# A hybrid decoder block on one core: the value products dealt out in three steps, and the state space kernels on four column tiles

## The chip, the cores and the metric

The program runs on one core of one Trainium2 chip. Its engines are TensorE (PE, with its weight load PEld), VectorE (DVE), ScalarE (ACT), GpSimd (POOL) and SyncE (SP, which starts most of the loads). The metric is the device time of one execution in microseconds. The kernel before takes 1155.02 us, the median of three runs (1151.35 to 1155.62).

## What is computed

The block takes 512 positions of width 1024, with 16 learned meta positions put in front (528 in all). Cut to what matters here:

```
h = concat(meta_tokens, x)
h = h + 0.5 * swiglu(rmsnorm(h), w1, w3, w2)              # first feed-forward
q, k, v, u, g_attn, g_ssm = split(rmsnorm(h) @ w_in)
attn = sliding_window_attention(q, k, v, sinks)           # 4 key groups x 4 query heads,
                                                          # blocks of 128, window 128, 16 meta keys
y    = s5_ssm(u, ...)                                     # 32 groups of 16 channels, 64 complex states
ssm  = (gelu(y) @ glu_a) * sigmoid(gelu(y) @ glu_b)
h = h + (sigmoid(g_attn) * attn + sigmoid(g_ssm) * ssm) @ w_out
h = h + 0.5 * swiglu(rmsnorm(h), ...)                     # second feed-forward
out = rmsnorm(h)[:, 16:]
```

In a query block of the attention, softmax runs over the 16 meta keys, up to 256 keys of the band and a sink; the value product is `p @ v` over those keys. The state space layer is computed in chunks of 8 steps; within a chunk its outputs come from a kernel of eight taps for each group, 16 by 16 channels each, which depends on the parameters alone.

## The kernel before

**Precision.** Weights and activations are split into a high and a low part (`whi`, `wlo`; `hgh`, `hgl`), and each large product is three matmuls for each 128 rows of the inner dimension (L238, L412, L414). ACT makes `whi` (L173) and DVE `wlo` (L174) from the weights as loaded (`raw`), in pieces of 128 output columns, by `prep_piece`. One piece feeds one *unit*: the 24 matmuls of 8 inner blocks. A unit's result (`p`) is taken out of PSUM by its evacuation, which is recorded in the next unit.

**Order.** Every engine runs its instructions in the order in which the program records them; nothing is scheduled behind it. Other work is put between a unit's matmuls by hand: `accumulate` takes a list of callbacks and runs them at equal distances in the unit. In the attention there are `NCUT = 11` such places in a unit, called cuts here and numbered 0 to 10; cut c stands behind matmul 2(c+1) of 24 (in a `glu` unit, which has two sums of 12, at about the same places).

**The state space kernels.** `ssm_params` is a generator whose steps run one in each unit of the first feed-forward. For each of four batches b of eight groups (`GB = 8`), it makes the kernel taps `Kt` (L651 to L658): for each group one matmul with the 128 x 16 stationary operand `BB` and the 128 x 128 moving operand `Qt` (L656), four of them into the rows 0 to 15 of one PSUM tile `psK`, side by side; one ACT copy of 16 x 512 (L658); then the same for the other four groups in the next step. Behind that POOL adds the diagonal (L663), and eight DMAs lay `Kt` out (L666).

**The attention.** Between projections, gates and glu units (30 units, table `MIX`) run 16 attention blocks n, key group k = n // 4 and query block b = n % 4. Block n begins in unit `BEGIN[n]`, and its parts stand in three units, at cuts given in the table `CUT`:
- In the first, `s1` for the four heads h at the cuts 2, 4, 7 and 7: two score matmuls `ps_s` (L1165, L1166), on DVE the mask and row minimum `mn` (L1168), on ACT the exponential `E` (L1170); behind head 3 the sum `den` and its reciprocal (DVE), and the scaling of `E` on POOL (L1181).
- In the second, at cut 7, `s2` turns the probabilities (`ps_t`, L1189; one or two sets of four) and splits them into `ph` (ACT, L1192) and `pl` (DVE, L1193). At cut 8, `s2m` turns the meta part (`ps_tm`, L1208), splits it (`ms`), and POOL spreads it into `m` (L1213). `prep_piece` is at cut 8 too, behind it.
- In the third, at cut 5, `s3` (L1217): the products of the band with `ph` and `pl` (L1224, two or four matmuls), the product of the meta part with `VM` (L1226), all into the PSUM tile `pv`; then ACT copies the lower half to `tb` (L1228), and DVE adds the halves into `AT` (L1230, two instructions).

The three parts of different blocks meet in one unit, in the order s3, s1, s2 where they share a cut. `ps_s` and `ps_tm` share two PSUM tiles, and `pv` has one:

```
1075    pt_ps = pool("ps_pt", 2, space=PSUM, c=ps3)
1076    pv_ps = pool("ps_pv", 1, space=PSUM, c=ps3)
```

Of the kernel before, what the change touches and what calls it, by code (L numbers as in the profile page):

```python
# [8 lines left out]
F32 = mybir.dt.float32  # L9
F32R = mybir.dt.float32r  # L10
AF = mybir.ActivationFunctionType
# [26 lines left out]
PREPS = (6, 34)  # L38
KS1 = 8
VS = (1, 0, 2, 10, 13, 13)  # L40
CUT = {"s3": 5, "s1": (2, 4, 7, 7), "s2o": 7, "s2p": 7, "s2m": 8, "prep": 8, "ev": 0, "ks": 10, "vs": 7}
BEGIN = (1, 2, 3, 4, 6, 7, 10, 11, 13, 14, 15, 18, 19, 20, 21, 24)

NG = 32
# [1 line left out]
GB = 8  # L46
NB = NG // GB
T = 8
# [17 lines left out]
def hybrid_block_kernel(  # L66
# [30 lines left out]
    V, S, G, PE, SY = nc.vector, nc.scalar, nc.gpsimd, nc.tensor, nc.sync  # L97
# [361 lines left out]
    Qt = pers.tile([128, NG, T + 1, 16], F32, name="Qt")  # L459
# [12 lines left out]
    def ssm_params(ps_p):  # L472
# [107 lines left out]
        ps = ps_p.tile([128, 512], F32, tag="ax", name="ps7")  # L580
# [13 lines left out]
        for i in range(2):  # L594
            ps = ps_p.tile([128, 512], F32, tag="ax", name="psA")
# [7 lines left out]
        BB = pp.tile([128, 2, NG, 16], F32, name="BB")  # L603
# [32 lines left out]
        for b in range(NB):  # L636
            gsl = slice(GB * b, GB * b + GB)
            tq = pp.tile([128, GB, T + 1, 16], F32, tag="s4", name="tq", bufs=2)
            G.tensor_tensor(out=Qt[:, gsl], in0=lam(LR, b, T + 1), in1=vec(A, 0, b, T + 1), op=ALU.mult)
            G.tensor_tensor(out=tq, in0=lam(LI, b, T + 1), in1=vec(A, 1, b, T + 1), op=ALU.mult)  # L640
            yield
            G.tensor_tensor(out=Qt[:, gsl], in0=Qt[:, gsl], in1=tq, op=ALU.add)
            Pb = pp.tile([128, GB, T, 16], F32, tag="s4", name="Pb", bufs=2)
            G.tensor_tensor(out=Pb, in0=lam(LR, b, T), in1=vec(BB, 0, b, T), op=ALU.mult)
            yield
            tq = pp.tile([128, GB, T, 16], F32, tag="s4", name="tq", bufs=2)
            G.tensor_tensor(out=tq, in0=lam(LI, b, T), in1=vec(BB, 1, b, T), op=ALU.mult)
            G.tensor_tensor(out=Pb, in0=Pb, in1=tq, op=ALU.add)
            yield
            yield  # L650
            Kt = pp.tile([16, GB, T, 16], F32, tag="s4", name="Kt", bufs=2)  # L651
            for h in range(2):
                ps = ps_p.tile([128, 512], F32, tag="ax", name="psK")
                for i in range(4):
                    g = GB * b + 4 * h + i
                    PE.matmul(out=ps[:16, 128 * i:128 * i + 128], lhsT=BB[:, 0, g, :],  # L656
                              rhs=Qt[:, g, 0:T, :].rearrange("p t c -> p (t c)"), start=True, stop=True)
                S.activation(out=Kt[:, 4 * h:4 * h + 4].rearrange("p g t c -> p (g t c)"), in_=ps[:16, :], func=AF.Copy)  # L658
                yield
            dg = pp.tile([16, GB, 16], F32, tag="dg", name="dg")  # L660
            G.tensor_tensor(out=dg, in0=ident[:16, 0:16].unsqueeze(1).to_broadcast([16, GB, 16]),
                            in1=dT[:, gsl].unsqueeze(2).to_broadcast([16, GB, 16]), op=ALU.mult)
            G.tensor_tensor(out=Kt[:, :, 0, :], in0=Kt[:, :, 0, :], in1=dg, op=ALU.add)  # L663
            for s in range(T):
                r0 = 16 * (T - 1 - s)
                G.dma_start(out=Mt[r0:r0 + 16, gsl, 16 * s:128],  # L666
                            in_=Kt[:, :, 0:T - s, :].rearrange("p g t c -> p g (t c)"))
            for h in range(2):
                ps = ps_p.tile([128, 512], F32, tag="ax", name="psW")
                for i in range(4):  # L670
                    PE.transpose(ps[:, 128 * i:128 * i + 128], Pb[:, 4 * h + i].rearrange("p t c -> p (t c)"), ident)
                S.activation(out=Wt[:, GB * b + 4 * h:GB * b + 4 * h + 4, :].rearrange("p g c -> p (g c)"), in_=ps, func=AF.Copy)
                yield
# [7 lines left out]
        for b in range(NB):  # L681
# [5 lines left out]
            n = 1  # L687
# [46 lines left out]
    ps = ax_ps.tile([128, 512], F32, tag="ax", name="ps_w")  # L734
    for _ in range(WARM):
        PE.matmul(out=ps[:, 0:128], lhsT=ones, rhs=ones, start=True, stop=True)
    ps = ax_ps.tile([128, 512], F32, tag="ax", name="ps_g")
# [106 lines left out]
    units, _ = ffn_units(hg, hT, True, mm_ps, g_p, t_p, CHUNKS1, norm_hook(t_p, hT, hg2, 1), first_mm)  # L844
# [237 lines left out]
    VM = a_p.tile([128, 4, 128], F32R, name="VM")  # L1082
# [5 lines left out]
    def tmp(name):  # L1088
        return a_p.tile([128, 512], F32, tag="t", name=name, bufs=4)
# [127 lines left out]
    def s3(n):  # L1217
        k, b = divmod(n, 4)
        _, _, tiles, ms = att.pop(n)
        pv = pv_ps.tile([128, 512], F32, tag="pv", name="pv")  # L1220
        first = True
        for ph, pl, kb in tiles:
            for p in (ph, pl):
                PE.matmul(out=pv, lhsT=VB[:, kb, k, :], rhs=p, start=first, stop=False)  # L1224
                first = False
        PE.matmul(out=pv, lhsT=VM[:, k, :], rhs=ms.rearrange("p h c -> p (h c)"), start=False, stop=True)  # L1226
        tb = tmp("tb")
        S.activation(out=tb[0:64], in_=pv[64:128, :], func=AF.Copy)  # L1228
        for e in range(2):
            V.tensor_tensor(  # L1230
                out=AT[64 * e:64 * e + 64, 2 * k:2 * k + 2, 128 * b:128 * b + 128],
                in0=pv[0:64].rearrange("p (i e c) -> p e i c", e=2, c=128)[:, e],
                in1=tb[0:64].rearrange("p (i e c) -> p e i c", e=2, c=128)[:, e], op=ALU.add)
# [57 lines left out]
    begin = dict(zip(BEGIN, range(16)))  # L1291
    for i, u in enumerate(units):
        cuts = [[] for _ in range(NCUT)]

        def at_cut(c, f, *a):
            cuts[c].append(lambda: f(*a))

        if i - 2 in begin:
            at_cut(CUT["s3"], s3, begin[i - 2])
        if i in begin:  # L1300
            for h in range(4):
                at_cut(CUT["s1"][h], s1, begin[i], h)
        if i - 1 in begin:
            for f, c in ((s2o, "s2o"), (s2p, "s2p"), (s2m, "s2m")):
                at_cut(CUT[c], f, begin[i - 1])
        at_cut(CUT["ev"], flush)
        if i == KS1:
            at_cut(CUT["ks"], ksplit, 1)
            at_cut(CUT["ks"], vmeta, 1)
        for v, iv in enumerate(VS):  # L1310
            if i == iv:
                at_cut(CUT["vs"], vsplit, *divmod(v, 3))
        at_cut(CUT["prep"], prep_piece)
        if i == len(units) - 2:
            mg += new_hg(SEQ)
            for m in range(6):
                at_cut(m, msplit, m)

        step(*u, mids=[lambda fs=fs: [f() for f in fs] for fs in cuts], prep=False, hold=i < len(units) - 1)
# [59 lines left out]
    n = CHUNKS2[-1]  # L1379
# [55 lines left out]
    ps = [new_p() for _ in range(2)]  # L1435
# [4 lines left out]
    for j in range(2 * ND):  # L1440
        h, d = divmod(j, ND)
        prep_piece()
        if j < 2:
            p = ps[j]
        else:
            p = new_p()
# [43 lines left out]
```

## Time and profile before

| what | value |
|---|---|
| three runs | 1151.35, 1155.02, 1155.62 us |
| the profiled execution's own time | 1151.97 us |
| its span, first to last instruction | 1150.2 us |
| granted TensorE clock, mean | 0.998 |
| busy: PE, PEld, DVE, ACT, POOL | 1130.5, 1006.9, 632.7, 408.8, 360.5 us |
| first feed-forward (span 0 to about 431 us) with the state space kernels | `psK` matmuls from 137.6 to 292.8 us |
| attention stage | about 510 to 716 us |

The profile is of one execution. Times are microseconds from the start of the span unless marked ns. "Busy" of PE is modelled at the matmul's end, since matmuls overlap, so starts are the safer reading: the pace of a stream is the distance from start to start. A plain float32 matmul shows as two records with a weight load each, a split (float32r) one as one. The waits view names the instruction that waited, the one that let it go, the total, the count and the longest.

### The profile page before, as it was taken

Reading aid. Unit: us, or ns where it says so; the run is one execution under the profiler, and the core shown is the slowest. Engines: PE = TensorE matmul, PEld = TensorE weight load, DVE = VectorE, ACT = ScalarE, POOL = GpSimd, SP = SyncE. Lnnn points to the kernel's source line nnn. Section 1 sums busy time; section 2 is a strip of 40 time slices with the busy share of each in tenths; the row PEclk is TensorE's granted clock in tenths of the full one; section 3 lists DMA queues with packets and bytes.
Section 4 is the critical chain, followed back from the end, with each engine's and each line's share of the span. In section 5 each row is a group of like instructions: output and inputs, shape, how many; then the busy total and the mean of one; then the engine's idle time right before and its main releaser. Section 6 shows DMA issues by size and latency. Waiting matters only on the chain.

```text
span 1150.2 us, 17220 instructions
## 1 busy us (share of the span) xinstructions
PE 1130.5 (98%) x7006; PEld 1006.9 (88%) x7006; DVE 632.7 (55%) x960; ACT 408.8 (36%) x719; POOL 360.5 (31%) x488
## 2 busy tenths in 40 slices
PE   9999999999999999999999999999999999999997
PEld 7999999999999999977777778888888888888887
DVE  5446653645444463877777776564544444444454
ACT  5322222232222242456555554343322321322234
POOL 2957672543685031444453331021000000000003
PEclk9999999999999999999999999999999999999999
DMA  6423233232423146122212222432323223323222
GB/s 186 99 90 107 74 93 109 77 85 83 111 74 102 62 141 204 49 74 74 72 45 69 74 74 74 147 110 74 128 92 110 74 83 120 112 70 126 76 74 74
DMA packets 105583, 108.43 MB, mean 94 GB/s; under 512 B 7504, under 2 KB 101968, under 8 KB 105376
## 3 DMA queue, kind: packets, MB, share of 16 engines
q1 hardware_dynamic: 103104, 100.74, 27.9%
q0 software_dynamic: 2352, 6.52, 2.2%
q8 instruction: 55, 0.90, 0.3%
q14 instruction: 24, 0.20, 0.1%
q10 hardware_dynamic: 48, 0.07, 0.0%
HBM read 100.80 MB, written 5.34 MB: 92 GB/s over the span
## 4 chain that ended last, share of the span: by engine, by line
PE 86%; DVE 5%; ACT 4%; issue 2%; POOL 2%; DMA 0%; POOLq 0%; DVEq 0%; SPq 0%; ACTq 0%
PE p L238 58%; PE p L412 11%; PE p L414 9%; PE p L798 1%; ACT E L1170 1%; PE p L1385 1%; POOL m L1213 1%; POOL E L1181 1%; DVE wlo L174 1%; PE psK L656 1%; ACT whi L173 1%; PE ps_x L744 1%; PE ps_t L1189 1%; ACT qs L1142 0%; PE pv L1224 0%
## 5 line engine op out<-in xcount | busy, mean ns | idle before, releaser
L238 PE MATMUL p<-hgh,whi 128*128 128x264 f32 (+1 forms) x1408 | 403.3, 333 | 0.1
L238 PE MATMUL p<-hgl,whi 128*128 128x264 f32 (+1 forms) x1408 | 402.3, 332 | 0.0
L238 PE MATMUL p<-hgh,wlo 128*128 128x264 f32 (+1 forms) x1408 | 400.6, 331 | 0.0
L174 DVE TENSOR_TENSOR wlo<-raw,whi 128x1024 fp32r<-128x1024 f32 (+2 forms) x192 | 256.4, 1336 | 105.0 <-ACT whi L173 102.7
L238 PEld LDWEIGHTS p<-hgh,whi 128*128 128x128 f32 x1408 | 238.6, 188 | 25.8 <-issue 1.5
L238 PEld LDWEIGHTS p<-hgh,wlo 128*128 128x128 f32 x1408 | 238.2, 188 | 23.4
L238 PEld LDWEIGHTS p<-hgl,whi 128*128 128x128 f32 x1408 | 238.4, 188 | 22.3
L173 ACT ACTIVATE whi<-raw 128x1024 fp32r<-128x1024 f32 (+2 forms) x192 | 187.5, 979 | 132.5 <-PE p L414 72.2
L1401 POOL TENSOR_TENSOR acc<-acc,zq 128x256 f32<-128x256 f32 x12 | 8.8, 735 | 349.9 <-ACT zq L1394 349.7
L384 ACT ACTIVATE t<-t 128x528 f32<-128x528 f32 (+1 forms) x44 | 28.1, 639 | 164.2 <-DVE t L383 164.2
L394 ACT ACTIVATE gh<-t 128x528 fp32r<-128x528 f32 (+1 forms) x44 | 28.1, 639 | 159.5 <-DVE t L393 159.5
L432 DVE SCALAR_TENSOR_TENSOR hT<-p,hT 128x528 f32<-128x528 f32 (+1 forms) x56 | 39.1, 698 | 82.8 <-PE p L414 52.2
L412 PE MATMUL p<-gh,whi 128*128 128x264 f32 x352 | 72.6, 288 | 0.7 <-DVE hT L432 0.5
L412 PE MATMUL p<-gl,whi 128*128 128x264 f32 x352 | 71.4, 284 | 0.0
L412 PE MATMUL p<-gh,wlo 128*128 128x264 f32 x352 | 71.3, 284 | 0.0
L383 DVE TENSOR_TENSOR t<-p,r_bc 128x528 f32<-128x528 f32 (+1 forms) x44 | 30.7, 698 | 70.5 <-PE p L238 67.4
L393 DVE TENSOR_TENSOR t<-p,t 128x528 f32<-128x528 f32 (+1 forms) x44 | 30.7, 698 | 64.3 <-PE p L238 63.9
L412 PEld LDWEIGHTS p<-gh,whi 128*128 128x128 f32 x352 | 54.5, 188 | 2.3 <-issue 1.2
L414 PE MATMUL p<-gh,whi 128*128 128x512 f32 x144 | 56.0, 389 | 0.0
L414 PE MATMUL p<-gl,whi 128*128 128x512 f32 x144 | 56.0, 389 | 0.0
L414 PE MATMUL p<-gh,wlo 128*128 128x512 f32 x144 | 56.0, 389 | 0.0
L1181 POOL TENSOR_TENSOR E<-E,den 128x512 f32<-128x512 f32 (+1 forms) x20 | 28.5, 1431 | 84.9 <-DVE den L1176 57.4
(322 smaller groups left out, 1516.4 us busy)
## 6 DMA issues: line engine op xcount, KB each, us to landing
raw<-in_ffn_w_dram SPq DMA_DIRECT2D x42, 1024.0 KB, 5.4
raw<-in_ffn_w_dram SPq DMA_DIRECT2D x24, 768.0 KB, 4.2
raw<-in_w_in_dram SPq DMA_DIRECT2D x16, 1024.0 KB, 5.3
raw<-in_ffn_w_dram SPq DMA_DIRECT2D x12, 512.0 KB, 3.5
raw<-in_w_out_dram SPq DMA_DIRECT2D x4, 1024.0 KB, 8.0
h_keep<-hT POOLq DMA_DIRECT2D x1, 2112.0 KB, 7.1
raw<-in_ssm_glu_a_dram SPq DMA_DIRECT2D x4, 512.0 KB, 3.5
raw<-in_ssm_glu_b_dram SPq DMA_DIRECT2D x4, 512.0 KB, 4.5
```

The costliest lines, as they stand in the source:

```text
L173: S.activation(out=hi, in_=src, func=AF.Copy)
L174: V.tensor_tensor(out=lo, in0=src, in1=fr(hi), op=ALU.subtract)
L238: PE.matmul(out=o, lhsT=w[:, k0 + k, :], rhs=sl(r, k), start=start, stop=stop)
L383: V.tensor_tensor(out=t1, in0=cell[1], in1=rb(), op=ALU.mult)
L384: S.activation(out=t1, in_=t1, func=AF.Silu)
L393: V.tensor_tensor(out=t3, in0=cell[3], in1=cell["t1"], op=ALU.mult)
L394: S.activation(out=gh, in_=t3, func=AF.Copy)
L412: PE.matmul(out=p[:, h, :HALF], lhsT=wt[:, k, :], rhs=gs[k][c][:, h, :], start=start, stop=stop)
L414: PE.matmul(out=p, lhsT=wt[:, k, :], rhs=gs[k][c].rearrange("p h c -> p (h c)"), start=start, stop=stop)
L432: V.scalar_tensor_tensor(out=hv(hT, d), in0=cell["p"], scalar=0.5, in1=hv(hT, d), op0=ALU.mult, op1=ALU.add)
L656: PE.matmul(out=ps[:16, 128 * i:128 * i + 128], lhsT=BB[:, 0, g, :], rhs=Qt[:, g, 0:T, :].rearrange("p t c -> p (t c)"), start=True, stop= ...
L1181: G.tensor_tensor(out=E[:, :, c:c + w], in0=E[:, :, c:c + w], in1=den.unsqueeze(2).to_broadcast([128, 4, w]), op=ALU.mult)
```

## The change

In the state space kernels, the eight groups of a batch now go into one PSUM tile, in one step: group 2j + i of the batch is put on column tile j (the 32 columns from 32j of the array, so the rows from 32j of PSUM), i beside i. Four ACT copies of 16 x 256 take the place of two of 16 x 512, two in this step and two in the next. The number of steps stays.

In the attention, `s3` is cut in three: the products of the band stay at cut 5 (`s3`), the product with `VM` goes to cut 7 (`s3m`, ahead of `s1` and `s2` there), and the copy `tb` and the sums `AT` go to cut 9 (`s3e`, behind `prep_piece` at cut 8). The PSUM tile `pv` and the number of instructions stay.

```diff
-CUT = {"s3": 5, "s1": (2, 4, 7, 7), "s2o": 7, "s2p": 7, "s2m": 8, "prep": 8, "ev": 0, "ks": 10, "vs": 7}
+CUT = {"s3": 5, "s3m": 7, "s3e": 9, "s1": (2, 4, 7, 7), "s2o": 7, "s2p": 7, "s2m": 8, "prep": 8, "ev": 0, "ks": 10, "vs": 7}
...
             Kt = pp.tile([16, GB, T, 16], F32, tag="s4", name="Kt", bufs=2)
-            for h in range(2):
-                ps = ps_p.tile([128, 512], F32, tag="ax", name="psK")
-                for i in range(4):
-                    g = GB * b + 4 * h + i
-                    PE.matmul(out=ps[:16, 128 * i:128 * i + 128], lhsT=BB[:, 0, g, :],
-                              rhs=Qt[:, g, 0:T, :].rearrange("p t c -> p (t c)"), start=True, stop=True)
-                S.activation(out=Kt[:, 4 * h:4 * h + 4].rearrange("p g t c -> p (g t c)"), in_=ps[:16, :], func=AF.Copy)
-                yield
+            ps = ps_p.tile([128, 512], F32, tag="ax", name="psK")
+            for i in range(2):
+                for j in range(4):
+                    g = GB * b + 2 * j + i
+                    PE.matmul(out=ps[32 * j:32 * j + 16, 128 * i:128 * i + 128], lhsT=BB[:, 0, g, :],
+                              rhs=Qt[:, g, 0:T, :].rearrange("p t c -> p (t c)"), start=True, stop=True, tile_position=(0, 32 * j), skip_group_check=True)
+            for j in range(4):
+                S.activation(out=Kt[:, 2 * j:2 * j + 2].rearrange("p g t c -> p (g t c)"), in_=ps[32 * j:32 * j + 16, 0:256], func=AF.Copy)
+                if j % 2:
+                    yield
...
             for p in (ph, pl):
                 PE.matmul(out=pv, lhsT=VB[:, kb, k, :], rhs=p, start=first, stop=False)
                 first = False
-        PE.matmul(out=pv, lhsT=VM[:, k, :], rhs=ms.rearrange("p h c -> p (h c)"), start=False, stop=True)
+        pvs[n] = (pv, ms)
+
+    pvs = {}
+
+    def s3m(n):
+        pv, ms = pvs[n]
+        PE.matmul(out=pv, lhsT=VM[:, n // 4, :], rhs=ms.rearrange("p h c -> p (h c)"), start=False, stop=True)
+
+    def s3e(n):
+        k, b = divmod(n, 4)
+        pv, _ = pvs.pop(n)
         tb = tmp("tb")
         S.activation(out=tb[0:64], in_=pv[64:128, :], func=AF.Copy)
         for e in range(2):
...
         if i - 2 in begin:
-            at_cut(CUT["s3"], s3, begin[i - 2])
+            for f, c in ((s3, "s3"), (s3m, "s3m"), (s3e, "s3e")):
+                at_cut(CUT[c], f, begin[i - 2])
```

How it moves instructions. PE in unit 4 of the attention, third part of block 1, before (`p` are the unit's own matmuls, `ps_s` the scores of block 3; in brackets the engines that an instruction waits for):

```order
L1224 MATMUL pv<-ph,VB 128x512 [waits Activation_49]
L1224 MATMUL pv<-pl,VB 128x512
L1224 MATMUL pv<-ph,VB 128x512 [waits Activation_49]
L1224 MATMUL pv<-pl,VB 128x512
L1226 MATMUL pv<-m_5997,VM 128x512 [waits Pool_49]
L238 MATMUL p<-YL,whi 128x512
L238 MATMUL p<-YH,wlo 128x512
L238 MATMUL p<-YH,whi 128x512
L238 MATMUL p<-YL,whi 128x512
...
L1165 MATMUL ps_s<-KH,qs 128x272 [waits DVE_49]
```

The same place in the changed kernel:

```order
L1226 MATMUL pv<-ph,VB 128x512 [waits DVE_49,PE_49,Activation_49]
L1226 MATMUL pv<-pl,VB 128x512
L1226 MATMUL pv<-ph,VB 128x512
L1226 MATMUL pv<-pl,VB 128x512
L238 MATMUL p<-YL,whi 128x512
...
L238 MATMUL p<-YL,whi 128x512
L238 MATMUL p<-YH,wlo 128x512
L238 MATMUL p<-YH,whi 128x512
L1234 MATMUL pv<-m_5997,VM 128x512 [waits Pool_49]
L1167 MATMUL ps_s<-KH,qs 128x272 [waits DVE_49]
```

The product with `VM` stands six matmuls later (four in units that are not `glu`), right ahead of the scores of heads 2 and 3. The first product of the band now waits for DVE as well as for ACT; so it does in ten of the 16 blocks, those whose predecessor has its third part in the unit before.

DVE in unit 3, where block 0 has its third part and block 2 its scores, from the masks of heads 0 and 1 to the next unit's first work, before:

```order
L1168 ISA mn 128x1
L1230 TENSOR_TENSOR AT<-pv,tb 64x2x128 x2
L1168 ISA E,mn<-ps_s,mC,sinkn 128x272
...
L1193 TENSOR_TENSOR pl<-ps_t,ph 128x512 x2
L1211 TENSOR_TENSOR ms<-ps_tm,ms 64x128
L174 TENSOR_TENSOR wlo<-raw,whi 128x1024
L1255 TENSOR_TENSOR ts<-p,r_bc 128x512
```

and in the changed kernel:

```order
L1195 TENSOR_TENSOR pl<-ps_t,ph 128x512 x2
L1213 TENSOR_TENSOR ms<-ps_tm,ms 64x128
L174 TENSOR_TENSOR wlo<-raw,whi 128x1024
L1242 TENSOR_TENSOR AT<-pv,tb 64x2x128 x2
L1267 TENSOR_TENSOR ts<-p,r_bc 128x512
```

The two sums `AT` have gone from ahead of the masks of heads 2 and 3 to behind `wlo`, the last work of the unit on DVE. On ACT, `tb` has gone from between the exponentials to behind `whi`.

## The prediction

> **What bounds the kernel now.** I read the page's busy times and chain first, then busy time by stage, then the waits of PE.
>
> ```profile
> PE 1130.5 (98%) x7006; PEld 1006.9 (88%) x7006; DVE 632.7 (55%) x960; ACT 408.8 (36%) x719; POOL 360.5 (31%) x488
> PE 86%; DVE 5%; ACT 4%; issue 2%; POOL 2%; DMA 0%; POOLq 0%; DVEq 0%; SPq 0%; ACTq 0%
> 167.00:319.00 152.00, 151.66 (x1235) 148.74 (x1234) 75.16 (x71) 40.81 (x54) 72.63 (x106) 1.00 0.32 93
> 510.00:716.00 206.00, 196.79 (x962) 158.70 (x962) 151.35 (x347) 113.88 (x277) 85.97 (x56) 1.00 0.21 67
> ```
>
> PE is busy 98% of the span, and the chain that ended last is 86% PE. In the first feed-forward (second number of a row: the stage; third: PE's busy time) PE stands still 0.3 us of 152: PE time taken out there comes out of the whole. In the attention PE idles 9 of 206 us, and DVE works 151: there PE and DVE hand over to each other, and each edit must be followed through both.
>
> **The state space kernels.** One burst of `psK`, with its neighbours on PE (start, length, name), the pace of the stream around it, and the groups of that tile:
>
> ```profile
> 137.38 0.28 PE L238 MATMUL p<-hgh,wlo 128*128 128x264 f32 x1
> 137.59 0.28 PE L656 MATMUL psK<-Qt,BB 128*16 128x128 f32 x1
> 138.37 0.27 PE L656 MATMUL psK<-Qt,BB 128*16 128x128 f32 x1
> 138.57 0.39 PE L238 MATMUL p<-hgh,whi 128*128 128x264 f32 x1
> 246.83 5.87 PE p L238 x48
> L656 PE MATMUL psK<-Qt,BB x64: 272/273/283, 137.6 to 292.8; 128*16 128x128 f32 x64
> L658 ACT ACTIVATE Kt<-psK x8: 587/588/589, 138.7 to 293.1; 16x512 f32<-16x512 f32 x8
> ```
>
> The stream's pace is 5.87 / 48 = 0.122 us. The burst's eight records (two for each float32 matmul) start over 0.78 us, 0.111 apart; going in costs 0.21 and coming out 0.20. So a burst takes 138.57 - 137.38 - 0.12 = 1.07 us of PE; eight of them (64 records) take 8.6 us.
>
> The change makes four bursts of 16 records on four column tiles. How far these run at once, the two-tile products `psY` tell, beside full-width transposes of the same 128 rows:
>
> ```profile
> 495.32 0.33 PE L999 MATMUL psY<-Mt,U 128*64 128x128 f32 x2
> 495.98 0.22 PE psY L999 x4
> 488.92 0.44 PE psT L1012 x4
> ```
>
> Four records take 0.22 us on two tiles and 0.44 on the whole array. Two that together span 0.33 us cannot have started more than some 0.01 apart, as one alone lasts about 0.32 after a start from rest: the tiles run side by side, each at a pace of 0.11.
> - Four at once: four rounds, starts over 3 x 0.11 + 0.02 = 0.35, and 0.21 + 0.35 + 0.20 - 0.12 = 0.64 us a burst. Saved: 8.6 - 4 x 0.64 = 6.0 us.
> - Two at once (in-order starts with two records to a matmul could allow no more): eight rounds, 0.21 + 0.78 + 0.20 - 0.12 = 1.07. Saved: 4.3.
> - None: 0.21 + 15 x 0.11 + 0.20 - 0.12 = 1.94. Saved: 0.8, four entries and exits.
>
> I take 5.4, between the first two and nearer to the first, because the two tiles start together with no sign of an order between them. [...] No row here shows four tiles.
>
> On ACT two copies of 0.59 give way to four of 256 columns; the nearest, `YH` of 128 x 256, takes 0.38. That is 0.35 us more for a batch, in a stage where ACT is busy 41 of 152 us, so I cost it at nothing; uncovered it would be 1.4 us.
>
> **The attention: what goes.** The waits in this stage (in total, times, longest), the first four of them on PE or its weight load:
>
> ```profile
> PE ps_s L1165 <- DVE mn L1168: 4.0, 3, 1.7
> PE pv L1226 <- POOL m L1213: 3.6, 7, 0.8
> PE ps_tm L1208 <- DVE mn L1168: 1.5, 3, 0.9
> PEld pv L1226 <- POOL m L1213: 7.5, 9, 1.3
> DVE AT L1230 <- ACT tb L1228: 20.8, 13, 2.6
> ```
>
> And block 0's third part, beside block 2's scores (unit 3), up to block 1's products:
>
> ```profile
> 529.26 0.39 PE L1224 MATMUL pv<-pl,VB 128*128 128x512 f32 x1
> 530.04 0.50 PE L1226 MATMUL pv<-m,VM 128*128 128x512 f32 x1 [0.39 <-POOL m L1213]
> 531.43 0.28 PE L1166 MATMUL ps_s<-KL,qs 128*128 128x272 f32 x1
> 532.01 0.85 DVE L1230 TENSOR_TENSOR AT<-pv,tb 64x256 f32<-64x256 f32 x2 [1.49 <-ACT tb L1228]
> 532.89 0.50 DVE L1168 CUSTOM_DVE_ANT_0 E<-ps_s,mC,sinkn 128x272 f32<-128x272 f32 x1
> 533.46 0.30 PE L1208 MATMUL ps_tm<-ident,pm 128*64 128x128 f32 x1 [0.16 <-DVE mn L1168]
> 536.95 1.41 DVE L174 TENSOR_TENSOR wlo<-raw,whi 128x1024 fp32r<-128x1024 f32 x1
> 537.82 0.39 PE L1224 MATMUL pv<-ph,VB 128*128 128x512 f32 x1
> ```
>
> *The stop at `VM`.* `m` is late: the start is 0.78 us behind the last, where 0.23 is usual. That is 0.55 lost, and the next matmul, its weights not preloaded, adds 0.1. Start to start, eight such stops and ten slow restarts come to 6.0 us; PE's idle time (3.6) and the load's (7.5) bracket it. The new place is four to six matmuls, 0.9 to 1.4 us, later. Only block 4's stop, 1.0 long in a stretch where POOL and ACT are late anyway, leaves some 0.6. So 5.4 goes.
>
> *The stop at `ps_tm`.* It waits for a mask that stands behind `AT` on DVE, which waits 1.5 us for `tb`. With `AT` gone from there, the three stops go: 2.0 us start to start (1.5 by the row).
>
> The three waits of `ps_s` stay: two lie ahead of the first `AT`, the third is below.
>
> **The attention: what comes.** `pv` has one PSUM tile, so block n+1's first product waits until block n's `AT` has read it. These sums now stand behind `wlo`. Unit 3: the second score matmul of head 2 ends at 531.71, so its mask can start at 531.75, 1.14 earlier than at 532.89. From mask to the end of `wlo` is a chain through DVE and ACT of 538.36 - 532.89 = 5.47 us, which stays. So `wlo` ends at 537.22 and `AT`, 0.87 behind, at 538.09, with `tb` done under `wlo`. PE comes there at 537.82 less the 0.32 of its `ps_tm` stop, 537.50 (the `VM` stop moves both alike). It stops for 0.59, plus 0.06 for the handover and 0.1 for the restart: 0.75 us. The next pair, and the one after it:
>
> ```profile
> 541.16 0.29 PE L1166 MATMUL ps_s<-KL,qs 128*128 128x272 f32 x1
> 542.17 0.50 DVE L1168 CUSTOM_DVE_ANT_0 E<-ps_s,mA,sinkn 128x272 f32<-128x272 f32 x1
> 546.23 1.26 DVE L174 TENSOR_TENSOR wlo<-raw,whi 128x1024 fp32r<-128x1024 f32 x1
> 546.64 0.39 PE L1224 MATMUL pv<-ph,VB 128*128 128x512 f32 x1
> 553.12 1.23 DVE L174 TENSOR_TENSOR wlo<-raw,whi 128x1024 fp32r<-128x1024 f32 x1
> 556.23 0.39 PE L1224 MATMUL pv<-ph,VB 128*128 128x512 f32 x1
> ```
>
> The mask starts 0.69 earlier, `AT` ends at 547.49 - 0.69 + 0.87 = 547.67, and PE is there at 546.64: 1.03 + 0.16 = 1.2 us. In the third pair `AT` ends at 555.2, ahead of 556.23: no stop. Gone through like this, eight of the ten pairs in neighbouring units stop for 0.5 to 1.2 us, 6.0 together.
>
> One more loss: around the first gates DVE itself is the chain.
>
> ```profile
> 579.79 1.90 DVE AT L1247
> 581.72 1.74 DVE AT L1238
> 584.25 1.50 DVE wlo L174
> 587.83 0.69 DVE AT L1238
> 589.00 0.39 PE ps_s L1165
> ```
>
> From 578 on DVE sets when PE resumes at 589.00, and block 4's `AT` (0.85), which before ran in DVE's idle time, now joins this chain. What PE gained just ahead is handed back; with a smaller case of the kind around block 7, 1.0 us.
>
> Sum for the attention: -5.4 - 2.0 + 6.0 + 1.0 = -0.4 us. Ends: -7.4 if the bank never holds PE, +5.6 if all ten pairs stop for 1.2.
>
> **The sum.** -5.4 - 0.4 = -5.8 us. The profiled execution took 1151.97 (span 1150.2 and 1.8 around it): 1146.2. The median of the runs stands 3.05 above that execution, so I predict 1149 for the median, 0.5% faster. About 0.5%, 5.8 us, is what a measurement of this kernel can tell from no change.
>
> **Rivals.** All on the median's scale.
> - *The bank is free in time*: the `VM` and `ps_tm` stops go and no others come. For it: PE has about 16 matmuls from cut 9 to the next cut 5. Against it: `wlo` ends past the next product's start in both pairs above, before `AT` is put behind it. 1155.0 - 5.4 - 7.4 = 1142.2. Chance 0.2.
> - *The column tiles run in pairs or one by one*, so that the change does not do what it says: -0.8 to -4.3, with the attention at -0.4: 1150.3 to 1153.8. For it: two records in series for each matmul. Against it: tiles that start together. Chance 0.2.
> - *The chain ahead of `AT` slows down*, and the one `pv` tile closes a loop: product, scores, mask, exponentials, `whi`, `wlo`, `AT`, next product. Its price is that of the chain's swings: `wlo` takes 1.23 to 1.41 above, but 1.90 is the length of another DVE operation of half that size when POOL works beside it. At 1.2 more in each of eight pairs the attention is +9.2, and with -5.4 the total +3.8: 1158.8, slower; from about 1.5 a pair it is past 0.5%. Against it: POOL's work moves along with DVE's. Chance 0.1.
> - *My forecast*: about four tiles at once, bank stops that eat the gain in the attention. 1145 to 1152 by itself. Chance 0.5.
>
> **How the numbers follow.** Range 1141.5 to 1155.5: it takes in the free bank at the low end and the tiles one by one at the high one, and leaves out the slow chain and what repeated runs scatter. Faster by over 0.5% (below 1149.2): the free bank, 0.2, and about half of the forecast: 0.46. Slower by over 0.5%: 0.07, most of the slow chain. Within: 0.47.
>
> **What would show it.** Right: a `psK` burst of 16 records whose starts lie within 0.3 to 0.5 us and 0.2 us on both sides; no wait of `VM` for `m` but block 4's; no wait of `ps_tm`; DVE's wait for `tb` nearly gone; and a new row, `pv` waiting for DVE `AT`, some eight times, of about 4 to 6 us. Wrong: starts of `psK` in pairs 0.11 apart over 0.8 us (the second rival); no row of `pv` on `AT` (the first); that row above 9 us, or longer `wlo` (the third). The sync at the first gates is wrong if PE resumes there earlier than before by more than what the state space kernels gave.

## The result, and the profile after

| | median of the runs, us | lowest to highest |
|---|---|---|
| before | 1155.32 (6 runs) | 1151.35 to 1156.49 |
| changed | 1147.95 (6 runs) | 1146.12 to 1151.06 |
| changed, second set, beside other runs of before | 1146.05 (6 runs) | 1144.44 to 1148.12 |
| changed, third set | 1146.16 (6 runs) | 1145.35 to 1149.01 |

The ratio to before is 0.9943, with a 95% interval of 0.9924 to 0.9963; in the second and third set it is 0.9914 (0.9900 to 0.9928) and 0.9944 (0.9925 to 0.9962). The change makes the kernel 0.6% faster by the first set (0.6 to 0.9% over the three); the median lies 1.05 us below the 1149 of the prediction. The profiled execution of the changed kernel took 1148.62 us, with a span of 1146.8 and a mean granted clock of 0.990.

Busy times and the chain that ended last, from the page of the changed kernel:

```profile
PE 1127.8 (98%) x7006; PEld 1006.2 (88%) x7006; DVE 636.5 (55%) x960; ACT 410.4 (36%) x727; POOL 357.1 (31%) x488
PE 88%; DVE 5%; ACT 4%; issue 2%; DMA 1%; POOL 0%; SPq 0%; DVEq 0%; POOLq 0%; ACTq 0%
```

PE still bounds the kernel. POOL has all but left the chain (it had 2%): PE's product with `VM` no longer waits for `m`, but for 0.07 us at block 4.

**The state space kernels.** One burst in the timeline of PE (start, length, name), and the groups of its tile:

```profile
139.38 0.40 PE L238 MATMUL p<-hgh,wlo 128*128 128x264 f32 x2
139.71 0.63 PE L656 MATMUL psK<-Qt,BB 128*16 128x128 f32 x16
140.27 0.51 PE L238 MATMUL p<-hgh,whi 128*128 128x264 f32 x2
...
L656 PE MATMUL psK<-Qt,BB x64: 272/273/283, 139.7 to 281.0; 128*16 128x128 f32 x64
L659 ACT ACTIVATE Kt<-psK x16: 373/377/381, 140.5 to 287.0; 16x256 f32<-16x256 f32 x16
```

The 16 records of a burst span 0.63 us together, where one alone lasts 0.27: their starts lie within 0.36. The second matmul ahead of them starts at 139.38 + 0.12 = 139.50 and the first behind at 140.27, so the burst takes 0.77 - 0.12 = 0.65 us of PE, four bursts 2.6 in place of 8.6.

**The attention.** The waits that answer to those of before (in total, times, longest):

```profile
PE ps_s L1167 <- DVE mn L1170: 4.5, 4, 2.0
PE pv L1226 <- DVE AT L1242: 4.1, 8, 0.9
DVE AT L1242 <- ACT tb L1240: 0.6, 1, 0.6
ACT tb L1240 <- PE pv L1234: 1.9, 4, 1.3
PEld pv L1226 <- issue: 5.5, 7, 1.2
```

No row of PE's `pv` waiting for `m` and none of `ps_tm` is left (PE's weight load still waits once for `m`, 0.5 us, at block 4), and DVE's wait for `tb` fell from 20.8 to 0.6. In their place stands a row that before did not have: eight first products of the band wait 4.1 us for `AT`, to get the one `pv` tile. The first two, in the timeline:

```profile
530.83 1.49 DVE L174 TENSOR_TENSOR wlo<-raw,whi 128x1024 fp32r<-128x1024 f32 x1
532.24 0.84 DVE L1242 TENSOR_TENSOR AT<-pv,tb 64x256 f32<-64x256 f32 x2
533.23 0.47 PE L1226 MATMUL pv<-ph,VB 128*128 128x512 f32 x1 [0.52 <-DVE AT L1242]
...
541.52 0.84 DVE L1242 TENSOR_TENSOR AT<-pv,tb 64x256 f32<-64x256 f32 x2
542.50 0.47 PE L1226 MATMUL pv<-ph,VB 128*128 128x512 f32 x1 [0.91 <-DVE AT L1242]
```

`AT` stands behind `wlo`, ends at 533.08 (532.24 + 0.84), and the product starts 0.15 later; in the next unit the same.

**Where the time went.** The starts of named matmuls in the traces give the length of each stretch. The table has the difference from the profiled execution of before, in us. The end of the first feed-forward is read at the first `ps_st`, the product that follows it; the gates are the stretch from the `VM` product of block 5 to that of block 6.

| stretch | changed | changed, second trace | changed, third trace | tiles alone | three steps alone |
|---|---|---|---|---|---|
| start to the first `psK` | +2.1 | +1.7 | -0.3 | +2.8 | -0.2 |
| first `psK` to the end of the first feed-forward | -6.0 | -6.0 | -6.3 | -6.2 | +0.2 |
| from there to the end, without the gates | -1.7 | -1.8 | -1.6 | +0.1 | -1.9 |
| first gates | +2.2 | +2.3 | +2.2 | 0.0 | +2.3 |

So the tiles give 6.0 to 6.3, the attention gives 1.6 to 1.9 and loses 2.2 to 2.3 at the first gates, and the start of the program, which the change does not touch, differs from execution to execution by up to 3 us.

**What is new: the clock at the first gates.** The ten microseconds from PE's restart there, of the changed kernel (stretch and length; for PE, PEld, DVE, ACT and POOL the busy time and, in brackets, the instructions; granted clock, DMA share, GB/s):

```profile
584.30:594.30 10.00, 10.00 (x47) 8.46 (x47) 6.22 (x21) 5.87 (x17) 3.02 (x2) 0.83 0.04 15
```

And of the kernel before:

```profile
589.00:599.00 10.00, 10.00 (x54) 8.49 (x55) 6.84 (x26) 7.25 (x23) 3.18 (x3) 1.00 0.13 46
```

PE is busy throughout in both, and runs seven matmuls fewer in the same time. The stop ahead of it is only 0.33 us longer than before (2.43 from start to start for 2.10), so 1.9 of the 2.24 us lost at the gates lie behind the stop. The last section shows the clock's fall in finer steps.

### The profile page after: what moved, and what is told of

Its sections match the earlier page's. It is cut to its first block, busy times and chain, and to the rows that moved or that the text cites. A ratio compares the mean times of both kernels' runs of the same rounds, so it can differ in the third digit from the quotient of the medians.

```text
span 1146.8 us, 17241 instructions
## 1 busy us (share of the span) xinstructions
PE 1127.8 (98%) x7006; PEld 1006.2 (88%) x7006; DVE 636.5 (55%) x960; ACT 410.4 (36%) x727; POOL 357.1 (31%) x488
## 4 chain that ended last, share of the span: by engine, by line
PE 88%; DVE 5%; ACT 4%; issue 2%; DMA 1%; POOL 0%; SPq 0%; DVEq 0%; POOLq 0%; ACTq 0%
PE p L238 59%; PE p L412 11%; PE p L414 9%; PE p L800 2%; PE pv L1226 1%; PE p L1398 1%; DVE wlo L174 1%; ACT whi L173 1%; PE ps_t L1191 1%; DVE AT L1242 1%; PE ps_s L1167 1%; ACT E L1172 1%; PE ps_s L1168 1%; DMA xb<-in_x_dram 1%; ACT qs L1144 0%
## 5 line engine op out<-in xcount | busy, mean ns | idle before, releaser
L385 DVE TENSOR_TENSOR t<-t,r_bc 128x528 f32<-128x528 f32 (+1 forms) x44 | 37.2, 846 | 32.4 <-ACT t L384 32.4
```

The costliest lines, as they stand in the source:

```text
L385: V.tensor_tensor(out=t1, in0=t1, in1=rb(), op=ALU.mult)
```

## The experiments

Three theories stood at the start. **A**, that of the prediction: the tiles give about 6 us, and the new wait for the `pv` tile takes back what the attention gains. **B**: the attention gave a good part by itself, and the tiles less. **C**: PE is held by DVE's work as a whole in this stage, so that a stop that is taken away turns up at another place.

### Tiles alone, steps alone, and the changed kernel again

The first kernel has the new `psK` part, and `s3` in one piece; the second the reverse. The third is the changed kernel once more.

Against the changed kernel, the first:

```diff
-        pvs[n] = (pv, ms)
...
+        PE.matmul(out=pv, lhsT=VM[:, k, :], rhs=ms.rearrange("p h c -> p (h c)"), start=False, stop=True)
...
-            for f, c in ((s3, "s3"), (s3m, "s3m"), (s3e, "s3e")):
-                at_cut(CUT[c], f, begin[i - 2])
+            at_cut(CUT["s3"], s3, begin[i - 2])
```

The second:

```diff
-            for i in range(2):
-                for j in range(4):
-                    g = GB * b + 2 * j + i
...
+            for h in range(2):
...
+                for i in range(4):
+                    g = GB * b + 4 * h + i
```

> The column tiles alone, the attention as before. Theory A (the tiles gave 6.0 us, and in the attention the new wait for the sums AT takes back what the stops at VM and ps_tm gave): 6.0 us less than before, ratio about 0.9948; bursts of psK of 0.56 us, the waits of the attention as before (pv for m some 3.6 us). Theory B (the attention's edit gave a good part of the gain): 3 to 4 us less, 0.9970.

> The three steps of the value products alone, psK as before. Theory A: no measurable change, ratio 0.9985 to 1.0010; PE waits for AT some eight times, about 4 us, and no longer for m or at ps_tm. Theory B: 3 to 4 us less, about 0.9970.

> The changed kernel once more, beside the others on one chip: 0.9924 to 0.9963 as measured. Theory A adds up: the gains of the tiles alone and of the three steps alone sum to this one's within 1.5 us. Theory C allows less than the sum.

Measured: tiles alone 1149.72 us (1148.71 to 1150.52), ratio 0.9943 (0.9930 to 0.9956). Steps alone 1153.91 (1151.36 to 1154.65), ratio 0.9977 (0.9964 to 0.9989). The waits of the first:

```profile
PE ps_s L1167 <- DVE mn L1170: 4.0, 3, 1.7
PE pv L1228 <- POOL m L1215: 3.7, 7, 0.9
PE ps_tm L1210 <- DVE mn L1170: 1.5, 3, 0.9
```

And of the second:

```profile
PE ps_s L1165 <- DVE mn L1168: 4.6, 4, 2.1
PE pv L1224 <- DVE AT L1240: 4.1, 8, 0.9
```

The changed kernel once more took 1146.05 us, ratio 0.9914 (0.9900 to 0.9928): a little below the 0.9924 to 0.9963 expected. By the medians of this set it gains 10.2 us, the two parts alone 6.5 + 2.3 = 8.8; they add up within the 1.5 us that A had. Each part brings its own rows and leaves the other's alone. The tiles are worth 6.5 us by the runs and 6.2 by the trace, as A has it, and not the 3 to 4 of B. For the steps alone the two measures differ: 2.3 us (1.3 to 4.2) by the runs, none by the trace (+0.3 at the end, from a start like that of the profiled execution of before). The ratio, 0.9977, lies outside what A had (0.9985 to 1.0010), though its interval reaches into it; the interval holds B's 0.9970 as well. The last section shows a cause that could part runs and trace: starts that differ by 3 us. Nine of the 17 runs of before in this set lie between 1156.18 and 1156.52, while the profiled execution of before, at 1151.97, lies near their lower end. Whether the steps alone give nothing or 2 us stays open.

### The sums one cut earlier

With `s3e` at cut 8 in place of 9, `tb` and `AT` come ahead of the meta part's split and of `wlo` on DVE. Nothing else changes.

```diff
-CUT = {"s3": 5, "s3m": 7, "s3e": 9, "s1": (2, 4, 7, 7), "s2o": 7, "s2p": 7, "s2m": 8, "prep": 8, "ev": 0, "ks": 10, "vs": 7}
+CUT = {"s3": 5, "s3m": 7, "s3e": 8, "s1": (2, 4, 7, 7), "s2o": 7, "s2p": 7, "s2m": 8, "prep": 8, "ev": 0, "ks": 10, "vs": 7}
```

> The changed kernel with tb and the sums AT at cut 8 instead of 9, so ahead of ms and wlo on DVE and of ms and whi on ACT. Theory A: AT ends some 1.7 us earlier (ms 0.28 and wlo 1.41 are no longer ahead of it), more than the longest stop of 1.07, so the wait of pv for AT goes; the five stops behind the first gates, 3.2 us, come out in full and the three ahead of them, 2.2 us, partly: 3 to 5 us less than the changed kernel, ratio to before about 0.991. Rival C (PE is held by DVE's work as a whole, and a stop only moves): the wait turns up at m or ps_s, and the ratio stays near 0.994.

> The kernel with the sums at cut 8 once more, beside the next one on one chip: by its earlier runs 1138.0 to 1144.0 us in two groups about 5 us apart.

Measured: 1138.72 us (1138.01 to 1143.98), ratio 0.9865 (0.9844 to 0.9886); again, in another set, 1138.66 (1137.86 to 1144.12), ratio 0.9885 (0.9862 to 0.9908). This beats both kernels, the changed one by 7.3 to 7.5 us, where 3 to 5 were expected. Its waits of PE in the attention shrink to one row; in the second trace:

```profile
PE ps_s L1167 <- DVE mn L1170: 3.6, 3, 1.5
```

The wait for the bank is gone and came up nowhere else: theory C falls. From the first score to the end the second trace is 8.3 us shorter than the changed kernel's third trace, the first 5.6. In this stretch the two differ at the first gates alone, which the next experiment takes up. Of the 8.3 us, 6.0 lie outside the gates, where the stops for the bank were, and 2.3 at the gates, which the expectation did not have.

### The splits of the second pair of key groups in another unit

In the kernel with the sums at cut 8, and in the changed kernel, the split of the second pair of key groups (ACT's copies `KH` and POOL's differences `KL`) was moved from unit 8 to unit 11.

```diff
-KS1 = 8
+KS1 = 11
```

> The kernel with the sums at cut 8 (1138.72 us), and with the splits of the second pair of key groups moved from unit 8 to unit 11 (KS1 = 11 for 8), so that POOL no longer writes those keys while DVE works its way to the first gates. In the kernel with the sums at cut 8, DVE's AT takes 1.91 and 1.75 us at 573.35 and 575.28, where 0.69 is usual without POOL beside it, and PE stands at the first gates for 2.4 us, the longest wait of ps_s; behind it the granted clock was 0.83 over 580 to 590. If DVE's long operations make that stop, and the stop the lower clock: the two sums take about 0.7 each, so 2.3 us of the chain go, the longest wait of ps_s falls below 0.5, the clock over 580 to 590 is 1.00, and the time falls by the stop (2.3) and the clock (1.2 to 1.9): 3.5 to 4.2 us, ratio about 0.983. If the stop is set by the chain of scores and gates and not by POOL: the wait stays about 2 us, or moves to unit 11, and the time stays within 1 us of the kernel with the sums at cut 8. If the clock falls there for another reason than the stop: the stop goes, the clock stays below 0.9, and about 2.3 us are gained.

> The sums at cut 8 and the splits in unit 11 once more. If the trace is right that the stop at the first gates and the clock behind it cost 4.1 us, its runs lie 2 to 4 us below those of the kernel with the sums at cut 8 beside it, group by group. If the earlier medians are right (1139.60 against 1138.72), the stop and the clock come and go from run to run with the sums at cut 8, and the move gives nothing that counts: within 1 us.

> The changed kernel with nothing but the splits of the second pair of key groups moved from unit 8 to unit 11. With the sums at cut 8 the same move took the stop at the first gates (2.79 us start to start) and the dip of the clock behind it out of the trace, 4.1 us between the value products of blocks 5 and 6, but not out of the median of the few runs. If stop and clock cost what the trace shows: 3 to 4 us less than the changed kernel beside it (about 1143 us), the row of pv waiting for AT unchanged at about 4 us. If POOL's work costs the same at its new place: no wait of ps_s above 1.6 at the gates, but new waits in unit 11, and the same time as the changed kernel within 1 us.

Measured, sums at cut 8 and splits moved: 1139.60 us (1139.39 to 1141.33), ratio 0.9871 (0.9845 to 0.9897), and again 1139.77 (1138.96 to 1139.90), ratio 0.9881 (0.9861 to 0.9902). The changed kernel with the splits moved: 1144.49 (1141.63 to 1145.80), ratio 0.9919 (0.9898 to 0.9940), beside 1146.16 without.

In the trace the move does what was expected. The window that holds the first gates, of the first trace of the sums at cut 8 without the move:

```profile
580.00:590.00 10.00, 7.61 (x30) 6.12 (x30) 6.64 (x19) 5.41 (x15) 3.02 (x2) 0.83 0.34 105
```

And with it:

```profile
580.00:590.00 10.00, 10.00 (x55) 8.43 (x55) 6.85 (x26) 7.24 (x24) 3.37 (x3) 1.00 0.13 44
```

And the wait that is left with it:

```profile
PE ps_s L1167 <- DVE mn L1170: 2.3, 2, 1.5
```

PE no longer stands at the gates, and the clock is whole. From the first score to the end this is 4.0 us less than in the first trace of the sums at cut 8, and 1.3 less than in the second. In the changed kernel the move takes 3.4 us out of the same stretch: 4.0 at the gates, less what it costs elsewhere, where a ninth product now waits for `AT` (that row is 4.4 us, 9 times).

In the medians it gives nothing with the sums at cut 8, and 1.7 us in the changed kernel. Two things lie between. First, the stop there is not the same in all executions. Without the move, the 11 runs of the two sets fall into two groups, seven from 1137.86 to 1139.24 and four from 1142.94 to 1144.12; with it all eight lie between 1138.96 and 1141.33. The two traces show one of each group; of the 5.9 us between them, 2.7 lie at the first gates and 3.3 ahead of the first `psK`. POOL and DVE ahead of the gates in the first (1143.98 us):

```profile
573.34 1.36 POOL L1119 TENSOR_TENSOR KL<-kT,KH 64x544 fp32r<-64x544 f32 x1
...
573.35 1.90 DVE L1259 SCALAR_TENSOR_TENSOR AT<-ta,AT 128x512 f32<-128x512 f32 x1 [0.70 <-ACT ta L1258]
```

And in the second (1138.07 us):

```profile
570.19 1.92 POOL L1119 TENSOR_TENSOR KL<-kT,KH 64x544 fp32r<-64x544 f32 x1
...
570.19 0.69 DVE L1259 SCALAR_TENSOR_TENSOR AT<-ta,AT 128x512 f32<-128x512 f32 x1 [0.70 <-ACT ta L1258]
```

Both start together, to 0.01 us; in the one DVE takes 1.90, in the other 0.69, and POOL takes 1.36 in the one and 1.92 in the other. The 1.2 us make PE's stop 2.79 or 1.66 (start to start), and behind the longer one the clock falls to the 0.83 above. Second, all three traces of kernels with the splits moved have the long start of the last section, and the second trace of the sums at cut 8 has the short one. So the stop and its clock cost what the trace shows, but, as far as two traces and the groups of the runs tell, only in part of the runs; the move makes the runs even rather than the median lower, and the ratio stays above the 0.983 expected. In the changed kernel it gains less than the 3 to 4 us expected. Why no trace with the moved splits has a short start was not settled.

### The sums later, and the sums earlier still

The first kernel records `tb` and `AT` in the next unit, behind its evacuation at cut 0 (block 15 excepted). The second has them at cut 7, right behind the product with `VM`.

```diff
-                at_cut(CUT[c], f, begin[i - 2])
+                if f is not s3e or begin[i - 2] == 15:
+                    at_cut(CUT[c], f, begin[i - 2])
...
+        if i - 3 in begin and begin[i - 3] != 15:
+            at_cut(CUT["ev"], s3e, begin[i - 3])
```

```diff
-CUT = {"s3": 5, "s3m": 7, "s3e": 9, "s1": (2, 4, 7, 7), "s2o": 7, "s2p": 7, "s2m": 8, "prep": 8, "ev": 0, "ks": 10, "vs": 7}
+CUT = {"s3": 5, "s3m": 7, "s3e": 7, "s1": (2, 4, 7, 7), "s2o": 7, "s2p": 7, "s2m": 8, "prep": 8, "ev": 0, "ks": 10, "vs": 7}
```

> The changed kernel with tb and the sums AT one unit later, behind the evacuation at cut 0 (block 15 excepted), so that the one tile of the value products comes free later still. If the bank wait costs what it shows (Theory A): it stood at 4.1 us in eight stops with the sums at cut 9 and at none with the sums at cut 8, a step of two matmuls pairs; two cuts and an evacuation later every one of the ten neighbouring pairs waits, each 1 to 1.5 us longer than now, so 14 to 20 us in the row of pv waiting for AT, and 8 to 16 us more than the changed kernel, ratio 1.000 to 1.007. If PE is held by DVE's amount of work and the stop is only its place (Theory C): the row grows but the waits of ps_s at the gates shrink, and the time stays within 2 us of the changed kernel.

> The changed kernel with tb and the sums AT at cut 7, directly behind the product with VM, ahead of the scores of heads 2 and 3 and of the meta part there. By Theory A the bank is free long before the next product, so no wait of pv for AT; but the mask of head 2 stands behind AT on DVE again, and AT waits for tb, so the three waits of ps_tm for mn come back (1.5 us by the row of the kernel before, 2.0 start to start) and DVE's wait for tb grows from 0.6 to above 10 us: 1 to 4 us slower than with the sums at cut 8, ratio 0.987 to 0.990. If only the wait for the bank counts: the same as with the sums at cut 8, 0.9865.

Measured, later: 1178.00 us (1176.77 to 1182.26), ratio 1.0206 (1.0180 to 1.0231), 30 to 32 us above the changed kernel, where 8 to 16 were expected. Its waits, and its windows with one dip of the clock and over the attention:

```profile
PE pv L1226 <- DVE AT L1242: 25.1, 10, 5.2
```

```profile
640.00:650.00 10.00, 6.82 (x23) 5.18 (x22) 2.92 (x4) 1.85 (x3) 4.91 (x4) 0.70 0.33 107
500.00:716.00 216.00, 186.44 (x877) 149.34 (x876) 141.04 (x326) 108.98 (x264) 82.36 (x55) 0.95 0.19 58
```

All ten neighbouring pairs wait now, as A had it, and C falls again. The sizes were missed: the waits come to 25.1 us, not 14 to 20, perhaps because a late `AT` also makes the block that waits for it late, which was not followed up; and the mean clock in this stage is 0.95, against 0.99 in the changed kernel. Over 216 us that is worth up to 9 us, an estimate. The same window of the changed kernel:

```profile
500.00:716.00 216.00, 207.30 (x1003) 167.31 (x1002) 157.00 (x355) 120.28 (x285) 86.34 (x57) 0.99 0.21 67
```

From the first score to the end the trace is 29 us longer: 21 of waits, and 8 for which the clock can account.

Earlier: 1145.23 us (1143.49 to 1147.80), ratio 0.9917 (0.9896 to 0.9938). Its waits:

```profile
PE ps_s L1167 <- DVE mn L1170: 4.4, 5, 1.5
PE ps_tm L1210 <- DVE mn L1170: 3.7, 5, 0.9
DVE AT L1242 <- ACT tb L1240: 28.3, 15, 3.6
```

No wait for the bank, but DVE stands 28.3 us for `tb` with the masks behind it, and `ps_tm` waits five times (3.7 us; 1.5 in the kernel before). So it is 6.5 us slower than at cut 8, more than the 1 to 4 expected. Of the places tried, the best for the sums is behind the mask of heads 2 and 3 and ahead of `wlo`, at cut 8.

### The order of the tiles in a burst

The two matmuls of a column tile are put behind one another, where the changed kernel goes round the four tiles.

```diff
-            for i in range(2):
-                for j in range(4):
+            for j in range(4):
+                for i in range(2):
```

> The changed kernel with the eight matmuls of a psK burst in another order: two matmuls on one column tile behind one another (four records), then the next tile, where the changed kernel goes round the four tiles. If each tile works its own queue whatever the order: starts still four together, a burst of 16 records in about 0.56 us of the chain. If the starts go in the order of recording: a matmul waits for the one ahead on its tile and holds back those behind, so that only neighbours on different tiles overlap: starts over 10 to 13 rounds of 0.11, a burst of 1.1 to 1.5 us, and about 2 to 4 us for the four bursts together.

Measured: 1149.41 us, one run. A piece of its chain (start, length, name), and below it that of the changed kernel:

```profile
140.71 0.58 PE psK L656 x16
...
139.78 0.56 PE psK L656 x16
```

The order in which the tiles are named costs 0.02 us a burst (0.58 for 0.56): these eight matmuls show nothing of the 1.1 to 1.5 us that were expected if a matmul that waits for its tile held back those behind it.

### The changed kernel a third time

It is the measure for the three kernels of the last set of runs: the sums at cut 8 again, with the splits moved, and the changed kernel with the splits moved.

> The changed kernel once more, as the measure for the three kernels beside it: about 1146 to 1148 us, a ratio of 0.991 to 0.995.

Measured: 1146.16 us, ratio 0.9944, as expected.

## Why the prediction was right

The time was 1149 and came out at 1147.95; the sum was -5.8 us on the profiled execution, and the trace has -6.0 + 0.5 = -5.5 between the first `psK` and the end (-5.7 in the third trace). That the sum comes so near is in part luck: the tiles gave 0.6 to 0.9 us more than was said and the attention 0.9 less, and the two errors cancel. The medians differ by 7.4 us, 1.9 more than the trace; starts that differ by up to 3 us could make that, which is not shown.

- **Tiles, -5.4: right in kind, a little small.** The burst takes 0.65 us, the 0.64 of the term "four at once"; the saving is 6.0 to 6.3. I had stayed between that and the term for pairs because no row showed four tiles. The 16 starts lie in four groups of four, within 0.02 us in a group and 0.11 from group to group (from 139.71, 139.83, 139.94 and 140.05), where the eight of before started one by one, 0.11 apart. The four copies on ACT (0.377 us each) cost nothing that is seen in this stretch.
- **The stops at `VM`, -5.4, and at `ps_tm`, -2.0: right.** Both rows are gone. At block 4 0.23 us are left, not 0.6, so the first term was -5.8.
- **The stops for the bank, +6.0 in eight of ten pairs: right.** There are eight. Beyond the usual pace of 0.23 they measure 0.68, 1.07, 0.46, 0.70, 0.49, 0.95, 0.70 and 0.34 from start to start, together 5.4, and eight slow restarts of 0.08 add 0.6: 6.0. The two that were worked out, 0.75 and 1.2, came to 0.76 and 1.15.
- **The first gates, +1.0: the step that was mis-sized, at +2.2.** That block 4's `AT` joins DVE's chain held. From the start of the `wlo` ahead of the gates to the score behind them, the chain grew from 589.00 - 576.39 = 12.61 us to 584.30 - 570.84 = 13.46, by the 0.85 of `AT`. The first row of that stretch in the chain of before, whose end the prediction shows:

```profile
576.39 0.03 DVE wlo L174
```

  And the chain of the changed kernel:

```profile
570.84 0.66 DVE wlo L174
...
572.85 0.41 DVE AT L1242
...
575.11 1.00 DVE AT L1259
576.11 0.02 issue
576.14 1.73 DVE AT L1250
577.87 2.30 DVE wlo L174
...
584.30 0.39 PE ps_s L1167
```

  But PE came to the gates earlier too, and its stop grew by 0.33 us alone; with 0.36 at block 8's scores, the smaller case around block 7, that is 0.7 of the 1.0. So by the sign that the prediction gave for this step it is wrong in part: counted from the first `psK`, PE resumes at the gates 6.8 us earlier than before, 0.8 more than the tiles gave (7.0 and 0.7 in the third trace), and what it had gained ahead was not all handed back there. The other 1.9 us of the 2.2 were lost behind the stop. The prediction treated a stop as worth its own length; here the clock fell to 0.83 behind the longer one, for which it had no term.
- **The attention as a whole, -0.4: +0.5 by the trace.** With the 0.36 at block 8's scores the terms come to -5.8 - 2.0 + 6.0 + 0.4 + 2.2 = +0.8, 0.3 above what the trace has.
- **The median.** I added 3.05 us for the way from the profiled execution to the median, the weakest term of the time. In the changed kernel the profiled execution took 1148.62 us, 2.4 more than the 1146.2 of the sum, of which 2.1 lie ahead of the first `psK`, and it stands 0.67 above its median, not 3.05 below. That 1149 came out within 1.1 us is luck to that extent.

*The rivals.* The free bank fell, since the wait is there; moved one cut, the sums make it true. Its price was -12.8 us on the profiled execution, and the second trace of the sums at cut 8 is 13.9 shorter, by a profiled execution with the same short start. Tiles in pairs fell with the burst of 0.65. The slower chain fell too: `wlo` takes 2.30 at the first gates, where POOL works beside it, but 1.49 at the first stop for the bank, where that rival had put its price.

## What to carry to other kernels

Where a unit of work is cut into steps to take waits off one engine, look for what the last step sets free: here one PSUM tile came free a `wlo` later, and one cut's difference in where it is read was worth 7 us, about as much as the whole change. A stop of the bounding engine need not be worth its length alone: here 1.9 of the 2.2 us lost at the gates lay behind a stop of 2.43, at a granted clock of 0.83. And where the starts of executions differ by more than the change is worth, compare stretches between the same two instructions in the traces beside the medians.

## What the runs showed of the hardware

**The clock fell behind some stops of PE and not behind others.** Behind the stop at the gates it is 0.83 or 0.84 over ten microseconds in five traces (three of the changed kernel, the three steps alone, the other tile order); the stop of the changed kernel is 2.43 from start to start. It is 0.83 too behind the 2.79 of the sums at cut 8. Behind the 2.10 of the kernel before and the 1.66 of the second trace of the sums at cut 8 it is 1.00. In the kernel with the sums later it is 0.57 over 585 to 590, 0.50 over 645 to 650 and 0.56 over 660 to 665; but from 690 to 700 it is 1.00, though PE idles 2.23 us of the first five. So how long PE idles does not decide alone.

The same traces show where the idle time lies. In those of before and of the changed kernel, the changes of the clock are whole multiples of 3.413 us apart: in the changed kernel it is 0.50 from 8.29 to 21.94 (13.65, or 4 of them), 1.00 up to the fall at 585.14 (563.20, or 165), and 1.00 again from 588.55 to 1141.51 (552.96, or 162); before it is 1.00 from 15.78 to 1145.59 (1129.81, or 331). Stretches of that length around the stop at the gates of the changed kernel, counted from the fall; and two stretches around a stop of the sums later behind which the clock stayed at 1.00:

```profile
581.73:585.14 3.41, 1.37 (x8) 0.82 (x7) 2.51 (x7) 1.49 (x4) 0.00 (x0) 1.00 0.87 280
585.14:588.55 3.41, 3.41 (x11) 2.74 (x10) 2.27 (x10) 2.80 (x9) 1.36 (x2) 0.50 0.00 0
588.55:591.96 3.41, 3.41 (x18) 2.88 (x17) 2.08 (x5) 1.25 (x3) 1.66 (x1) 1.00 0.00 0
...
531.31:534.72 3.41, 1.86 (x10) 1.25 (x8) 2.11 (x3) 1.22 (x2) 2.36 (x2) 1.00 0.20 38
534.72:538.13 3.41, 2.46 (x11) 2.05 (x12) 1.72 (x6) 1.12 (x4) 0.00 (x0) 1.00 0.79 269
```

The clock is 0.50 for one stretch, with 11 matmuls where the next has 18, and whole again; half the clock over 3.41 us is 1.7 us, an estimate, near the 1.9 lost. In the stretch that ends with the fall PE idles 3.41 - 1.37 = 2.04 us. In no other stretch of the attention, in these two traces, does it idle more than the 1.71 of the stretch from 585.81 to 589.22 in the kernel before, at the gates, behind which the clock stayed at 1.00. The stop of the sums later leaves 1.55 and 0.95 in its two stretches. But ahead of 8.29, where the clock of the changed kernel falls too, PE idles only 0.74 us of 3.41. So whether the idle time of such a stretch decides is not shown. If it does in this stage, a stop of one length could cost the clock in one execution and not in the next, since the stretches lie elsewhere in each: the rises at 15.78 and 21.94 are 1.8 of them apart.

**POOL and DVE: of two instructions that started together, one took longer.** The two pairs of rows above show it: the one takes 1.36 (POOL) or 0.69 (DVE) and the other 1.90 (DVE) or 1.92 (POOL), nearly as long as both one after the other (1.36 + 0.69 = 2.05). Why, no run here shows. At starts that are equal to 0.01 us, which of the two took longer differed between two executions of one program, and with it the length of the stop at the gates (2.79 or 1.66) and the clock behind it (0.83 or 1.00), 2.7 us together.

**The start differs by 3 us and more, and the moment at which the clock rises differs too.** Ten microseconds near the start of the changed kernel:

```profile
10.00:20.00 10.00, 10.00 (x38) 7.65 (x38) 6.99 (x14) 7.38 (x16) 0.00 (x0) 0.50 0.60 174
```

And in its third trace:

```profile
10.00:20.00 10.00, 10.00 (x52) 7.83 (x52) 8.06 (x16) 7.12 (x16) 0.00 (x0) 1.00 0.60 173
```

Of the same program, 38 matmuls run in one execution and 52 in the other, and the first `psK` comes 2.4 us later in the one. The 1.00 of the view does not tell the clock there: it stands over 10.00 to 15.70 of the kernel before too, where the products `p` of 264 columns last 0.42 us (median), as they do in the changed kernel just ahead of the rise at 21.94. Behind 15.78 in the one and 21.94 in the other they last 0.28 or 0.29. So by its matmuls the clock of the kernel before rose at about 15.8, 6.2 us ahead of that of the changed kernel, and its first `psK` comes at 137.59, against 139.71. Of the 14 traces, those with more matmuls in the first 30 us come to the first `psK` earlier:

| matmuls in the first 30 us | first `psK`, us | traces |
|---|---|---|
| 164 | 136.3 | 1 (the sums at cut 7) |
| 158 or 159 | 137.3 to 137.6 | 4 (before, changed third, three steps alone, sums at cut 8 second) |
| 144 and 147 | 139.3 to 139.7 | 2 (changed first and second) |
| 134 to 138 | 140.3 to 140.9 | 7 (the others) |

The kernel before has one trace, with an early rise; its medians in the three later sets were 1156.24, 1155.67 and 1153.91. What sets the moment of the rise was not tried.
